# Merge gate logits of layer 2: projected in 128-column blocks inside the stick-breaking heads

## The chip, the cores and the metric

The kernel runs on 1 core of a Trainium2 chip. Its time is the device time of one launch in microseconds. Times quoted as "us from the start" are positions in one profiled execution. Engines are named as the profile names them: PE (TensorE matmuls), DVE (VectorE), ACT (ScalarE), POOL (GpSimd), SP (the queue that issues the DMAs).

## The reference, cut to what matters

Two transformer layers over 1024 tokens of width 1024, in float32. Only layer 2 is touched:

```
h = rms_norm(x)
sb_q, sb_k, sb_v, sb_g, r_q, r_k, r_v, r_g, m_sb, m_ret = split(h @ w_in)   # 10 x 1024 columns
out_a = stick_breaking(norm(sb_q), norm(sb_k), sb_v) * silu(sb_g)           # 8 heads of 128
out_b = norm(chunkwise_retention(rot(r_q), rot(r_k), r_v)) * silu(r_g)      # 4 heads of 256
merged = sigmoid(m_sb + b0) * (out_a @ w_branch_sb) + sigmoid(m_ret + b1) * (out_b @ w_branch_ret)
x = x + merged @ w_out
```

The merge gate logits are `m_sb` and `m_ret` with their biases: 2048 columns of the input projection. They depend on `h` alone and are needed only when the branches are merged.

## The kernel before

Every float32 product is made of three matmul passes over a rounded part and a rest of both operands (`PASSES`), so a block of 128 columns over 512 tokens takes 8 x 3 = 24 matmuls. Weights come in eight tiles of 128 rows (`split_unit`): a DMA into `raw` (three buffers), then POOL makes the rounded part (L70) and the rest (L71) in `wu` (ten buffers). Projection sums land in three PSUM banks named `acc`.

Layer 2 goes in five steps. **Heads:** for each of 8 stick-breaking heads, `dense_tok` projects q, k, v of 8 token tiles (L102, 192 matmuls 384 wide) and `dense_col` the gate (L112, 48 matmuls 512 wide). Then come 12 score blocks of a head (`pz`, L1025), each followed by a long elementwise chain over ACT, DVE and POOL (L1028 to L1048), transposes of the weights (`pt`, `pp`, L1055) and the value products (`po`, L1060). **Logits 0:** `merge_logits(0)` projects the first 512 of the 2048 logit columns, adds the bias on ACT (L956) and stores them in DRAM (`d_sg`). **Retention:** for each of 4 heads a projection (`ret_proj`) and a recurrence over 8 chunks (`ret_chain`, L1132 to L1187), which works on chunk 1 only after chunk 0. **Logits 1 to 3:** the other 1536 columns. **Merge:** `gated` multiplies the heads' outputs with their gates (L1201 to L1215, 16 half tiles through two buffers `ga` and two `oa`), `w_branch_sb` is applied (`acc<-oah,wu`), the same for retention, then `w_out`.

The order in which an engine takes its instructions is fixed when the program is built: a scheduler lists them by priority in the order in which they are written, and where an operand isn't ready in its model it takes later work first. Each engine then runs its own list strictly in order, so a waiting instruction holds up those behind it. A pool's memory is handed to a later pool only when the tiles that lie there are released. `gated` uses pools made after the retention's pool `rt` is closed.

Of the kernel before, what the change touches and what calls it, by code (L numbers as in the profile page):

```python
# [11 lines left out]
F32 = mybir.dt.float32  # L12
F32R = mybir.dt.float32r
AF = mybir.ActivationFunctionType
ALU = mybir.AluOpType
AX = mybir.AxisListType
PSUM = bass.MemoryType.PSUM
DRAM = bass.MemoryType.DRAM

P = 128  # L20
T = 1024
# [6 lines left out]
def f32(ap):  # L28
    return ap.bitcast(F32)
# [7 lines left out]
def tile_kernel(ctx: ExitStack, tc: tile.TileContext, I: dict, out: bass.AP, dbg=None, stop=None):  # L37
    nc = tc.nc
# [20 lines left out]

    # ---------------------------------------------------------------- helpers  # L60
    def split_unit(src, ncol, pool=None, tag="wu", parts=1, fast=False, rpool=None):
# [66 lines left out]
    def dve_transpose(dst, src):  # L128
        """dst[c, x, r, t] = src[t, x, r, c], 128 by 128 for every x and r, in blocks of 32 by 32"""
        for a in range(4):  # L130
            for b in range(4):
                nc.vector.transpose(out=dst[32 * b:32 * b + 32, :, :, 32 * a:32 * a + 32],  # L132
                                    in_=src[32 * a:32 * a + 32, :, :, 32 * b:32 * b + 32])
# [40 lines left out]
    def drain(g):  # L174
        for _ in g:
            pass

    def take(g, n):
        for _ in range(n):
            if next(g, None) is None:  # L180
                return
# [5 lines left out]

    # DRAM scratch
    d_pk = dram.tile([2, NM, P, 4, 4, P], F32, name="d_pk")
# [12 lines left out]

    # ---------------------------------------------------------------- layer 1: norm
    hT = join(new_halves("h1", 0), new_halves("h1", 1))
# [26 lines left out]

    # constants
    conv_w = load_const("conv_w", [P, 12, 5])
# [5 lines left out]
    dnw = load_const("dn_norm_w", [P, P], src=I["dn_norm_w"].partition_broadcast(P))  # L239
    # ---------------------------------------------------------------- layer 1: dz + gates  # L240
    gates = sm.tile([P, NM, 16], F32, name="gates")
# [23 lines left out]

    # gate scalars, [token in chunk, dir*4+head, chunk]
    gt = gates.rearrange("p m (d c h) -> p d c h m", d=2, c=2)
# [30 lines left out]

    # ---------------------------------------------------------------- layer 1: delta heads
    dn_ = tc.tile_pool(name="dn", bufs=1, side="right")  # L300
# [3 lines left out]
    for h in range(4):  # L304
# [5 lines left out]
        for b in range(3):  # L310
# [13 lines left out]
            sT.append(s)  # L324
        # q: raw, with its norm per token
        sq = dc.tile([P, T], F32, tag="cv", name="sq", bufs=2)
# [6 lines left out]
        nc.vector.tensor_scalar_mul(out=rq[:, h, :], in0=rq[:, h, :], scalar1=P ** -0.5)  # L333
        # k: token major, normalized, and back
        ks = dn.tile([P, NM], F32, tag="ks", name="ks", bufs=2)
# [31 lines left out]
        for d in range(2):  # L367
# [12 lines left out]

            # decay [s, c]: with its diagonal for the products with q, strictly above it for the system
            # (the backward system is stored transposed)
            def decay(a, b, sgn, strict, tag):
# [11 lines left out]
            else:  # L395
# [17 lines left out]
                for g in range(2):  # L413
# [5 lines left out]
                    for dd_, E in enumerate((E0, E1)):  # L419
# [3 lines left out]
                        nc.sync.dma_start(out=d_pk[dd_, g * 4:g * 4 + 4, :, 3, h, :].rearrange("n p c -> p n c"), in_=IT)  # L423
        # operands of the scan
        for d in range(2):
# [21 lines left out]

    # ---------------------------------------------------------------- layer 1: inverses of the 64-blocks
    naB = tc.tile_pool(name="naB", bufs=1, side="right")
# [26 lines left out]

    # ---------------------------------------------------------------- layer 1: neighbourhood attention

    def na_proj(p, hold):
# [13 lines left out]
        for m, acc in dense_tok(hT, us, 0, 384):  # L493
            j = m % 4
            sq = na1.tile([P, 256], F32, tag="sq", name="sq", bufs=2)
            nc.scalar.activation(out=sq, in_=acc[:, 0:256], func=AF.Square)
            ss = na1.tile([P, 4], F32, tag="ss", name="ss", bufs=2)
            nc.vector.tensor_reduce(out=ss, in_=sq.rearrange("p (h d) -> p h d", h=4), op=ALU.add, axis=AX.X)
            rsqrt_small(ss, ss, 1.0 / 64, EPS, 4)
            kn = na1.tile([P, P], F32, tag="kn", name="kn", bufs=5)  # L500
            nc.scalar.copy(out=qn[:, m, :], in_=acc[:, 0:128])
            nc.scalar.copy(out=kn, in_=acc[:, 128:256])
            nc.scalar.copy(out=v[:, m, :], in_=acc[:, 256:384])
            for x, t_ in enumerate((qn[:, m, :], kn)):
                t_ = t_.rearrange("p (h d) -> p h d", h=2)
                nc.vector.tensor_tensor(out=t_, in0=t_, in1=ss[:, 2 * x:2 * x + 2].unsqueeze(2).to_broadcast([P, 2, 64]),
                                        op=ALU.mult)
            kns.append(kn)
            if j == 3:
                sl = slice((m - 3) * P, (m + 1) * P)  # L510
                # head 0 keeps its rounded part above the rest, head 1 the other way round
                pt = bank("a")
                for jj, k_ in enumerate(kns):
                    nc.tensor.transpose(pt[:, jj * P:(jj + 1) * P], k_, ident)
                for hh in range(2):
                    a, b = slice(hh * 64, hh * 64 + 64), slice(64 - hh * 64, 128 - hh * 64)
                    nc.scalar.activation(out=kS[hh][a, sl], in_=pt[a, :], func=AF.Copy, scale=gk[a])
                    nc.vector.scalar_tensor_tensor(out=kS[hh][b, sl], in0=pt[a, :], scalar=gk[a],  # L518
                                                   in1=f32(kS[hh][a, sl]), op0=ALU.mult, op1=ALU.subtract)
                kns = []  # L520
            yield 1
# [4 lines left out]
    def na_attn(p, tiles):  # L526
        qn, kS, v, z, TB = tiles[p]

        def scores(t, hh, st):
# [24 lines left out]
            if rl != ru:  # L554
                # the second row's window starts one row later: its last row takes the place of the first
                nc.tensor.matmul(ps[64:128, 0:64], lhsT=q2[:, hh, :], rhs=f32(kS[hh][:, (rl + 8) * 64:(rl + 9) * 64]),
                                 start=True, stop=True)
# [92 lines left out]

    # ---------------------------------------------------------------- layer 1: delta rule scan
    sc_ = tc.tile_pool(name="sc", bufs=1)
# [191 lines left out]

    # ---------------------------------------------------------------- layer 1: output (transposed), layer 2: norm
    # the tokens in two sets: the inner 512, which the scan leaves first, and the outer 512
    def token_set(ap, s):
# [33 lines left out]
    h2T = new_hT(hp2, "h2")  # L881
# [57 lines left out]

    # ---------------------------------------------------------------- layer 2: stick breaking attention  # L940
    NOSYNC = mybir.DependencyInfo(mybir.DependencyClass.NoSync, mybir.DependencyReason.DATA)
# [8 lines left out]

    def merge_logits(q):
        us = load_units(I["w_in_2"], 8192 + 512 * q, 512)
        for b in range(4):
            for half, acc in enumerate(dense_col(h2T, us, b * P)):
                lg = mp.tile([P, 512], F32, tag="lg", name="lg", bufs=2)
                nc.scalar.activation(out=lg, in_=acc, func=AF.Identity, bias=bm[:, 4 * q + b:4 * q + b + 1])  # L956
                nc.sync.dma_start(out=d_sg[4 * q + b, :, half * 512:half * 512 + 512], in_=lg)

# [5 lines left out]
    last_sb = None  # L964
    with tc.tile_pool(name="sb", bufs=1) as sb, tc.tile_pool(name="sr", bufs=1, side="right") as sr:
        gqk = sr.tile([P, 2, P], F32, name="gqk")
# [3 lines left out]
        for h in range(8):  # L970
# [43 lines left out]
            for ib in (0,1):  # L1014
                po = bank("o")
                ini = sb.tile([P, 4], F32, tag="ini", name="ini", bufs=2)
                for diag in ((True, False) if ib else (True,)):
                    c0 = ib * 512 if diag else 0
                    As = []
                    for i4 in range(4):  # L1020
# [27 lines left out]
                        last_sb = nc.scalar.activation(out=A[:, :w], in_=A[:, :w], func=AF.Exp)  # L1048
                        As.append(A)
                    for kb in range(4):  # L1050
                        i0 = kb if diag else 0
# [12 lines left out]
                nc.vector.tensor_copy(out=ov, in_=po)  # L1064
                nc.sync.dma_start(out=d_oa[h, :, ib * 512:ib * 512 + 512], in_=ov)
    if "oa" in dbg:
        nc.sync.dma_start(out=dbg["oa"], in_=d_oa)
    if stop == "E":
        return

    merge_logits(0)

    # ---------------------------------------------------------------- layer 2: retention
    d_ob = dram.tile([8, P, T], F32, name="d_ob")
    d_gb = dram.tile([8, P, T], F32, name="d_gb")
    with tc.tile_pool(name="rt", bufs=1) as rt:
# [45 lines left out]
        def ret_chain(h, tiles):  # L1122
            qTs, kTs, vs = tiles
            state = None
            for g in range(2):
                qT, kT, v = qTs[g], kTs[g], vs[g]
                # scores^T of four chunks
                psc = bank("z")
# [60 lines left out]
        for h in range(4):  # L1189
            ret_chain(h, ret_proj(h))  # L1190
    for q in range(1, 4):
        merge_logits(q)
    if stop == "F":
        return

    # ---------------------------------------------------------------- layer 2: branches and merge
    d_mg = dram.tile([8, P, T], F32, name="d_mg")
# [134 lines left out]
```

## Time and profile before

| | |
|---|---|
| runs | 2332.72 us median of 3 (2330.21 to 2334.63) |
| span of the profiled execution, first to last instruction | 2331.9 us |
| PE busy | 2182.4 us, 94% |
| DVE busy | 1414.8 us, 61% |
| ACT busy | 863.7 us, 37% |
| POOL busy | 1252.0 us, 54% |
| mean granted TensorE clock | 0.981 of full |

Of the profiled execution its span is given; what lies around it is within the spread of the three runs. PE's busy time counts a matmul from its start to its modelled end. Matmuls overlap: one 512 wide is shown as 0.39 us long, but the next starts 0.23 us after it. So PE's true idle time is larger than its share suggests, and it is found by counting matmuls and multiplying with the distance between starts.

### The profile page before, as it was taken

The numbers are of one execution on the slowest core, as the hardware profiler recorded it, in microseconds if no ns is written. First come the engines' busy times: TensorE is split into PE (matmuls) and PEld (weight loads), VectorE is DVE, ScalarE is ACT, GpSimd is POOL, SyncE is SP. The second block draws the span as 40 slices with busy tenths as digits, with TensorE's granted clock in tenths as the row PEclk, the third lists the DMA queues.
The fourth block names the chain that finished last, engine by engine and source line by source line (L and its number), as shares of the span: only waits on it lengthen the run. The fifth ranks groups of instructions, "written<-read, shape, count | busy, mean of one in ns | idle before, by whom it ended". The sixth has DMA issues, their size and how long they took to land.

```text
span 2331.9 us, 33715 instructions
## 1 busy us (share of the span) xinstructions
PE 2182.4 (94%) x12069; PEld 1864.4 (80%) x12069; DVE 1414.8 (61%) x2596; ACT 863.7 (37%) x2126; POOL 1252.0 (54%) x1467
## 2 busy tenths in 40 slices
PE   7998888999999999899889999999999999989999
PEld 7776877787888798787788777788888888767887
DVE  4688789844456568887877784426474744343221
ACT  5344334445554235554555544112222222332210
POOL 6667778851004256565565664536363633666531
PEclk9999999999999999999999999999999999999999
DMA  4266820154475421111011112211111122666433
GB/s 131 80 170 166 203 80 26 37 165 132 154 279 205 153 84 46 50 55 55 10 50 50 55 50 72 72 56 46 64 46 64 46 82 91 226 213 211 140 109 108
DMA packets 236488, 240.86 MB, mean 103 GB/s; under 512 B 39776, under 2 KB 173600, under 8 KB 236064
## 3 DMA queue, kind: packets, MB, share of 16 engines
q1 hardware_dynamic: 236320, 238.71, 32.5%
q8 instruction: 95, 1.56, 0.3%
q14 instruction: 73, 0.60, 0.1%
HBM read 167.31 MB, written 71.34 MB: 102 GB/s over the span
## 4 chain that ended last, share of the span: by engine, by line
PE 33%; DVE 16%; POOL 7%; issue 4%; DMA 4%; ACT 4%; SPq 0%; POOLq 0%; ACTq 0%; DVEq 0%
PE acc L112 21%; PE acc L102 5%; DVE qf L132 4%; PE acc L859 3%; DVE A L1039 3%; POOL A L1044 2%; DMA raw<-in_w_in_dram 1%; POOL wu L71 1%; DVE A L1035 1%; POOL ss L126 1%; DMA oa<-d_oa 1%; DVE ob L132 1%; DVE sq L988 1%; DVE wT L1058 1%; PE pt L1160 1%
## 5 line engine op out<-in xcount | busy, mean ns | idle before, releaser
L112 PE MATMUL acc<-h2h,wu 128*128 128x512 f32 x1504 | 459.1, 396 | 6.7 <-DVE sq L988 2.7
L102 PE MATMUL acc<-wu,h2h 128*128 128x384 f32 (+1 forms) x1536 | 376.2, 327 | 13.4 <-DVE sq L988 4.2
L71 POOL TENSOR_TENSOR wu<-raw,wu 128x512 fp32r<-128x512 f32 (+3 forms) x268 | 363.4, 1365 | 6.3
L70 POOL TENSOR_SCALAR wu<-raw 128x512 fp32r<-128x512 f32 (+3 forms) x268 | 205.9, 772 | 250.7 <-PE acc L112 176.7
L112 PEld LDWEIGHTS acc<-h2h,wu 128*128 128x128 f32 x1504 | 281.5, 188 | 71.9 <-ACT lg L956 3.1
L102 PEld LDWEIGHTS acc<-wu,h2h 128*128 128x128 f32 x1536 | 272.2, 194 | 21.5 <-issue 3.5
L112 PE MATMUL acc<-h2l,wu 128*128 128x512 f32 x752 | 276.1, 396 | 0.0
L102 PE MATMUL acc<-wu,h2l 128*128 128x384 f32 (+1 forms) x768 | 250.1, 327 | 0.0
L102 PE MATMUL acc<-wu,h1hi 128*128 128x384 f32 (+2 forms) x768 | 193.1, 335 | 12.6 <-DVE kS L518 6.7
L112 PE MATMUL acc<-h1hi,wu 128*128 128x512 f32 x512 | 164.3, 409 | 8.0 <-ACT pad L315 4.7
L112 PEld LDWEIGHTS acc<-h2l,wu 128*128 128x128 f32 x752 | 141.4, 188 | 31.0
L102 PEld LDWEIGHTS acc<-wu,h1hi 128*128 128x128 f32 x768 | 138.5, 196 | 17.0 <-issue 8.0
L1044 POOL TENSOR_TENSOR A<-Z,A 128x128 f32<-128x128 f32 (+2 forms) x96 | 112.4, 1176 | 70.5 <-DVE A L1039 43.6
L102 PEld LDWEIGHTS acc<-wu,h2l 128*128 128x128 f32 x768 | 148.4, 193 | 1.0
L102 PE MATMUL acc<-wu,h1lo 128*128 128x384 f32 (+2 forms) x384 | 127.8, 335 | 0.0
L112 PEld LDWEIGHTS acc<-h1hi,wu 128*128 128x128 f32 x512 | 98.1, 193 | 33.0 <-ACT pad L315 6.2
L126 POOL TENSOR_TENSOR ss<-ss,mhalf 128x2 f32<-128x2 f32 (+2 forms) x136 | 115.6, 851 | 7.2
L132 DVE STREAM_TRANSPOSE qf<-sq 32x256 f32<-32x256 f32 x256 | 111.6, 436 | 4.0
L125 POOL TENSOR_SCALAR ss<-ss 128x2 f32<-128x2 f32 (+2 forms) x136 | 42.5, 312 | 117.7 <-ACT sq L982 47.0
L1060 PE MATMUL po<-wT,v 128*128 128x512 f32 (+3 forms) x288 | 76.1, 365 | 22.2 <-DVE wT L1058 12.2
L112 PE MATMUL acc<-h1lo,wu 128*128 128x512 f32 x256 | 96.4, 405 | 0.0
L112 PE MATMUL acc<-oah,wu 128*128 128x512 f32 x256 | 81.3, 413 | 10.0 <-DVE sg L1232 6.1
(547 smaller groups left out, 4770.5 us busy)
## 6 DMA issues: line engine op xcount, KB each, us to landing
raw<-in_w_in_dram SPq DMA_DIRECT2D x192, 256.0 KB, 2.8
d_pk<-sct SPq DMA_DIRECT2D x24, 512.0 KB, 4.3
raw<-in_w_out_dram SPq DMA_DIRECT2D x40, 256.0 KB, 2.8
wsa<-d_pk SPq DMA_DIRECT2D x16, 512.0 KB, 6.0
wsb<-d_pk SPq DMA_DIRECT2D x16, 512.0 KB, 7.1
d_sg<-lg SPq DMA_DIRECT2D x32, 256.0 KB, 2.6
sg<-d_sg SPq DMA_DIRECT2D x32, 256.0 KB, 4.3
raw<-in_w_in_dram SPq DMA_DIRECT2D x32, 192.0 KB, 2.7
```

Source lines behind the costliest of these rows:

```text
L70: nc.gpsimd.tensor_scalar(out=u[:, 0, :], in0=raw, scalar1=1.0, scalar2=0.0, op0=ALU.mult, op1=ALU.add)
L71: nc.gpsimd.tensor_tensor(out=u[:, 1, :], in0=raw, in1=f32(u[:, 0, :]), op=ALU.subtract)
L102: nc.tensor.matmul(acc[:, :n], lhsT=hT[a][:, k, m * P:(m + 1) * P], rhs=us[k][:, b, c0:c0 + n], start=(k == 0 and i == 0), stop=(k == NK - ...
L112: nc.tensor.matmul(accs[half], lhsT=us[k][:, b, c0:c0 + P], rhs=hT[a][:, k, half * 512:(half + 1) * 512], start=(k == 0 and i == 0), stop= ...
L125: nc.gpsimd.tensor_scalar(out=dst, in0=src, scalar1=mul, scalar2=eps, op0=ALU.mult, op1=ALU.add)
L126: nc.gpsimd.tensor_tensor(out=dst, in0=dst, in1=mhalf[:, :eshape], op=ALU.pow)
L132: nc.vector.transpose(out=dst[32 * b:32 * b + 32, :, :, 32 * a:32 * a + 32], in_=src[32 * a:32 * a + 32, :, :, 32 * b:32 * b + 32])
L859: nc.tensor.matmul(acc, lhsT=us[k][:, y, (b % 4) * P:(b % 4 + 1) * P], rhs=token_set(mT[x][:, k, 0:T], s), start=(k == 0 and i == 0), stop ...
L988: nc.vector.scalar_tensor_tensor(out=sq[:, a * P:(a + 1) * P], in0=acc[:, a * P:(a + 1) * P], scalar=ss[:, a:a + 1], in1=gqk[:, a, :], op0 ...
L1039: nc.vector.tensor_tensor_scan(out=A[:, :w][:, ::-1], data0=A[:, :w][:, ::-1], data1=A[:, :w][:, ::-1], initial=0.0 if diag else ini[:, i4 ...
L1044: nc.gpsimd.tensor_tensor(out=A[:, :w], in0=Z[:, :w], in1=A[:, :w], op=ALU.subtract)
L1060: nc.tensor.matmul(po[:, i0 * P:512], lhsT=v[a][:, c0 // P + kb, :], rhs=wT[b][:, :n], start=(diag and kb == 0 and x == 0), stop=(diag == ...
```

## The change

`merge_logits` becomes a generator over 16 blocks of 128 columns. A block loads its weights in two DMAs of 4 row tiles (`fraw`, two buffers), splits them on POOL (`fu`, three buffers, L960 and L961 of the new file) and yields after each half of 512 tokens. Every head asks for one half after the scores of each of its three groups of four blocks, 24 halves in all; the other 8 follow after the last head. Both former calls are gone. The same edit sets the size of a scratch reserve (`dynamic_dma_scratch_size`) to 1024. The count of matmuls is the same.

```diff
-    def merge_logits(q):
-        us = load_units(I["w_in_2"], 8192 + 512 * q, 512)
-        for b in range(4):
-            for half, acc in enumerate(dense_col(h2T, us, b * P)):
+    def merge_logits():
+
+        for b in range(16):
+            cols = slice(8192 + b * P, 8192 + (b + 1) * P)
+            us = []
+            for g in range(2):
+                raw = fp.tile([P, 4, P], F32, tag="fraw", name="fraw", bufs=2)
+                nc.sync.dma_start(out=raw, in_=I["w_in_2"][g * 512:(g + 1) * 512, cols].rearrange("(k p) c -> p k c", p=P))
+                u = fp.tile([P, 2, 4, P], F32R, tag="fu", name="fu", bufs=3)
+                nc.gpsimd.tensor_scalar(out=u[:, 0], in0=raw, scalar1=1.0, scalar2=0.0, op0=ALU.mult, op1=ALU.add)
+                nc.gpsimd.tensor_tensor(out=u[:, 1], in0=raw, in1=f32(u[:, 0]), op=ALU.subtract)
+                us += [u[:, :, k, :] for k in range(4)]
+            for half in range(2):
+                acc = dense_half(h2T, us, 0, half)
                 lg = mp.tile([P, 512], F32, tag="lg", name="lg", bufs=2)
-                nc.scalar.activation(out=lg, in_=acc, func=AF.Identity, bias=bm[:, 4 * q + b:4 * q + b + 1])
-                nc.sync.dma_start(out=d_sg[4 * q + b, :, half * 512:half * 512 + 512], in_=lg)
+                nc.scalar.activation(out=lg, in_=acc, func=AF.Identity, bias=bm[:, b:b + 1])
+                nc.sync.dma_start(out=d_sg[b, :, half * 512:half * 512 + 512], in_=lg)
+                yield 1
...
+        fill = merge_logits()
...
                         last_sb = nc.scalar.activation(out=A[:, :w], in_=A[:, :w], func=AF.Exp)
                         As.append(A)
+                    take(fill, 1)
...
+        drain(fill)
...
-    merge_logits(0)
...
-    for q in range(1, 4):
-        merge_logits(q)
...
-    nc = _bacc.Bacc("TRN2", target_bir_lowering=False, num_devices=1)
+    nc = _bacc.Bacc("TRN2", target_bir_lowering=False, num_devices=1, dynamic_dma_scratch_size=1024)
```

How it stands on PE in the scores of a middle head, before: between the score blocks `pz` lie projections of the next head (`acc<-wu`, 384 wide).

```order
L1025 MATMUL pz<-qkt 128x256 x3
L1025 MATMUL pz<-qkt 128x384 x3
L102 MATMUL acc<-wu,h2h 128x384
L102 MATMUL acc<-wu,h2l 128x384
L102 MATMUL acc<-wu,h2h 128x384 x2
L102 MATMUL acc<-wu,h2l 128x384
L1055 MATMUL pt<-ident,A 128x128
L1055 MATMUL pp<-ident,A 128x128
L102 MATMUL acc<-wu,h2h 128x384
```

The same place after the change: between the score blocks lie the logit matmuls (`acc<-h2h,fu`).

```order
L1038 MATMUL pz<-qkt 128x384 x3
L120 MATMUL acc<-h2h,fu 128x512
L120 MATMUL acc<-h2l,fu 128x512
L120 MATMUL acc<-h2h,fu 128x512 x2
L120 MATMUL acc<-h2l,fu 128x512
L120 MATMUL acc<-h2h,fu 128x512 x2
L1038 MATMUL pz<-qkt 128x512 x3
L120 MATMUL acc<-h2l,fu 128x512
L120 MATMUL acc<-h2h,fu 128x512 x2
L120 MATMUL acc<-h2l,fu 128x512
L120 MATMUL acc<-h2h,fu 128x512
L1069 MATMUL pt<-ident,A 128x128
```

The logits stand among the scores, and most of the next head's projection now stands behind them, among the value products.

On PE at the end of the last retention head, before: logits (`acc<-h2h,wu`) lie between the state products (`po<-v,kd`) and the outputs of a chunk (`pt<-v,wT` and `pt<-ss,qs`).

```order
L1171 MATMUL po<-v,kd 128x256 x6
L112 MATMUL acc<-h2l,wu 128x512
L112 MATMUL acc<-h2h,wu 128x512 x2
L112 MATMUL acc<-h2l,wu 128x512
L112 MATMUL acc<-h2h,wu 128x512 x2
L112 MATMUL acc<-h2l,wu 128x512
L112 MATMUL acc<-h2h,wu 128x512
L1152 MATMUL pt<-v,wT 128x256 x3
L1160 MATMUL pt<-ss__18692,qs 128x256
```

The same after the change, up to the first matmul on the gated output `oah`.

```order
L1173 MATMUL pt<-ss__19488,qs 128x256
L1173 MATMUL pt<-ss__19489,qs 128x256
L1173 MATMUL pt<-ss__19488,qs 128x256 x2
L1173 MATMUL pt<-ss__19489,qs 128x256
L1173 MATMUL pt<-ss__19488,qs 128x256
L1165 MATMUL pt<-v,wT 128x256 x3
L1173 MATMUL pt<-ss__19519,qs 128x256
L1173 MATMUL pt<-ss__19520,qs 128x256
L1173 MATMUL pt<-ss__19519,qs 128x256 x2
L1173 MATMUL pt<-ss__19520,qs 128x256
L1173 MATMUL pt<-ss__19519,qs 128x256
L112 MATMUL acc<-oah,wu 128x512
```

The logits between the chunks of the last retention head, and between it and the first branch matmul, are gone.

On SP after the change, where the loads of the first gated half tiles (`ga`, `oa`) stand: behind the last stores of the retention's outputs (`d_ob`), as before the change, but now with the branch weights already loaded ahead of them.

```order
L64 DMA raw<-in_w_branch_sb_dram 128x512 x5
L1200 DMA d_ob<-ob 128x512 x4
L1218 DMA ga<-d_ga 128x512
L1219 DMA oa<-d_oa 128x512
L1218 DMA ga<-d_ga 128x512
L1219 DMA oa<-d_oa 128x512
```

The gating still starts only when the last retention head has ended.

## Rows read from the trace of the kernel before

**Rows 1.** Windows by step: span, busy (and count) by engine, clock, DMA share, GB/s

```profile
886.50:1451.10 564.60, 513.62 (x2679) 450.22 (x2678) 441.74 (x847) 288.55 (x832) 336.30 (x439) 0.98 0.15 45
...
1890.00:1981.50 91.50, 91.50 (x446) 76.20 (x446) 40.14 (x73) 22.49 (x48) 37.22 (x47) 1.00 0.27 91
1981.50:2063.00 81.50, 73.23 (x306) 56.34 (x304) 32.82 (x33) 29.38 (x48) 56.04 (x47) 1.00 0.64 213
2063.00:2149.50 86.50, 79.76 (x318) 62.33 (x319) 38.38 (x47) 27.78 (x45) 48.61 (x40) 0.94 0.65 216
2149.50:2331.90 182.40, 178.69 (x768) 143.70 (x766) 36.57 (x50) 19.08 (x31) 72.75 (x71) 1.00 0.36 124
```

**Rows 2.** PE's groups from 886.5 to 1451.1 us: count, busy, mean ns, idle before

```profile
L102 PE MATMUL acc<-wu,h2h 128*128 128x384 f32 x860 | 234.1, 346 | 9.3 <-DVE sq L988 3.6 <-DVE wu L68 2.5 <-ACT gv L1012 2.3
...
L112 PE MATMUL acc<-h2h,wu 128*128 128x512 f32 x350 | 109.9, 397 | 2.7 <-DVE sq L988 2.7
L1060 PE MATMUL po<-wT,v 128*128 128x512 f32 (+3 forms) x288 | 76.1, 365 | 22.2 <-DVE wT L1058 12.2 <-ACT wT L1057 4.5 <-DVE ov L1064 1.7
L1025 PE MATMUL pz<-qkt 128*128 128x512 f32 (+3 forms) x288 | 71.3, 358 | 10.0 <-ACT Z L1028 7.8 <-ACT qkt L999 2.1
...
L1055 PE MATMUL pt<-ident,A 128*128 128x128 f32 x160 | 33.8, 282 | 6.8 <-ACT A L1048 6.7
```

**Rows 3.** PE's timeline at three places: start, length of the run, its count

```profile
1166.09 0.69 PE L102 MATMUL acc<-wu,h2h 128*128 128x384 f32 x3
...
1888.37 1.95 PE L1132 MATMUL pz<-ro 128*128 128x128 f32 x16
...
2077.24 1.10 PE L112 MATMUL acc<-oah,wu 128*128 128x512 f32 x4
```

**Rows 4.** PE's timeline in the last retention head, two chunks

```profile
1909.52 0.51 PE L1152 MATMUL pt<-v,wT 128*128 128x256 f32 x3
...
1917.80 0.52 PE L1152 MATMUL pt<-v,wT 128*128 128x256 f32 x3
```

**Rows 5.** DVE's and POOL's timeline in the same head

```profile
1913.28 0.55 DVE L1165 TENSOR_SCALAR ot<-pt,rdv,ss 128x256 f32<-128x256 f32 x1 [0.45 <-POOL ss L126]
...
1922.13 7.18 DVE L132 STREAM_TRANSPOSE ob<-ot 32x256 f32<-32x256 f32 x16
...
1932.87 7.18 DVE L132 STREAM_TRANSPOSE kf<-ro 32x256 f32<-32x256 f32 x16 [0.24 <-DMA d_ob<-ob]
...
1970.45 7.19 DVE L132 STREAM_TRANSPOSE ob<-ot 32x256 f32<-32x256 f32 x16
...
1912.30 0.94 POOL L126 TENSOR_TENSOR ss<-ss,mhalf 128x1 f32<-128x1 f32 x1
```

**Rows 6.** Instructions on tile oa: ns min/median/max, first and last start

```profile
L1209 POOL TENSOR_TENSOR oa<-oa,ga x32: 1271/1297/1793, 1985.9 to 2137.0; 128x512 f32<-128x512 f32 x32
L1213 DVE TENSOR_TENSOR oa<-oa,ga x32: 691/781/1699, 1987.9 to 2139.0; 128x512 f32<-128x512 f32 x32
...
L1214 ACT CAST oah<-oa x16: 612/620/623, 1988.6 to 2060.7; 128x512 fp32r<-128x512 f32 x16
```

**Rows 7.** DMA issues from 1980 to 2070 us: median us to landing

```profile
oa<-d_oa SPq DMA_DIRECT2D x16, 256.0 KB, 3.4
```

**Rows 8.** A window at the start of the retention, columns as in rows 1

```profile
1510.00:1520.70 10.70, 8.35 (x40) 7.95 (x40) 8.74 (x18) 1.66 (x2) 3.83 (x4) 0.53 0.17 51
```

**Rows 9.** PE's timeline in that window, at half clock

```profile
1516.41 0.41 PE L102 MATMUL acc<-wu,h2l 128*128 128x256 f32 x1
1516.62 0.63 PE L102 MATMUL acc<-wu,h2h 128*128 128x256 f32 x2
```

**Rows 10.** POOL's weight splits on the page: mean ns, idle before

```profile
L71 POOL TENSOR_TENSOR wu<-raw,wu 128x512 fp32r<-128x512 f32 (+3 forms) x268 | 363.4, 1365 | 6.3
L70 POOL TENSOR_SCALAR wu<-raw 128x512 fp32r<-128x512 f32 (+3 forms) x268 | 205.9, 772 | 250.7 <-PE acc L112 176.7
```

More of the change, by code (lines that the diff above doesn't have):

```diff
@@ L964, in tile_kernel @@
     last_sb = None
-    with tc.tile_pool(name="sb", bufs=1) as sb, tc.tile_pool(name="sr", bufs=1, side="right") as sr:
+    with tc.tile_pool(name="fp", bufs=1) as fp, tc.tile_pool(name="sb", bufs=1) as sb, \
+            tc.tile_pool(name="sr", bufs=1, side="right") as sr:
+        fill = merge_logits()
         gqk = sr.tile([P, 2, P], F32, name="gqk")
```

## Prediction

> **What bounds the kernel now.** I read the page first: PE is the busiest engine, DVE second, and the end of the chain of waits is mostly PE. Then the windows by step, because the change moves work from two steps into a third. The reader is to see in them that the steps have different limits [rows 1]: in the heads (886.5 to 1451.1 us) PE is shown busy for 513.62 of 564.60 us while DVE works 441.74, or 78%; in the last retention head (1890.0 to 1981.5) PE is busy all the time and DVE 44%; in the gating (1981.5 to 2063.0) PE still has 73.23 of 81.50 us. The PE work of those last two windows is for the most part logits 1 to 3.
>
> Then the groups of PE in the heads, to count the matmuls [rows 2]: 860 on `h2h` 384 wide, with half as many on `h2l` (two passes of three read `h2h`), so 1290; 350 and half as many 512 wide, some 524; 288 each of `po`, `pz` and transposes. Their distance comes from runs in the timeline [rows 3]: four 512 wide take 1.10 us, one alone 0.40, so 0.233 each; three 384 wide 0.69 against 0.34, so 0.175; sixteen 128 wide 1.95, so 0.11. Of `po` and `pz` half are 512 wide and a sixth each 384, 256 and 128 (256 wide: 0.117, from three in 0.51 us against 0.28 for one [rows 4]). The sum is 1290 x 0.175 = 226, 524 x 0.233 = 122, 2 x (144 x 0.233 + 48 x (0.175 + 0.117 + 0.11)) = 106 and 288 x 0.11 = 32, together 486 us. So PE waits 564.6 - 486 = 79 us in this step. That is what the change can win there.
>
> The groups also tell where PE waits [rows 2]. Of 51 us shown idle, 22.2 stand ahead of `po` (for the weights `wT` of DVE and ACT), 10.0 ahead of `pz`, 6.8 ahead of `pt`, 12.0 ahead of projections.
>
> **The change part by part.** *What moves.* 32 halves of 24 matmuls, 768, at 0.233: 179 us of PE. 192 of them (logits 0, 45 us) already lie in the window of the heads and still do, as the eight halves drained at the end. The other 576, or 134 us, come from beside the last retention head and the gating into the heads. No matmul is added or dropped.
>
> *The heads get longer.* They grow by 134 us less what falls into the 79 us of waiting. The bounds are 134 - 79 = 55 (every wait filled) and 134 (none). In the new order the logits lie between the score blocks, and the projections behind them among the value products. So the waits ahead of `pz` and `pt` get cover; those ahead of `po` lie among the same neighbours as before. I let the share of `po` stay: 79 x 22.2 / 51 = 34 us. The projection waits go, since most stood behind DVE, whose 442 us would then lie in some 654 (67%). The heads grow by 134 - 79 + 34 = 89 us.
>
> *The last retention head loses its cover.* What is left is the recurrence itself, and it gets faster, because PE no longer runs logits between its links. A chunk took 8.28 us from one `pt` to the next [rows 4]. Its links are the nine matmuls from 1909.52, ACT's square, POOL's root until 1913.24 and DVE's `ot` until 1913.83 [rows 5], when the bank is free again: 4.4 us. The transposes of DVE between the two halves of the sequence and at the end (7.18 us three times [rows 5]) stay as they are. In the first half three steps save 3.9 us each, so its last `ot` would end at 1910 and not at 1922, where the transposes follow it. From there to the first state of the second half I keep the 25 us of before (two rows of transposes, the store between them, the split of `kd`). The last three chunks save 10: two steps, and some 2 us in which the first of them stood behind logits. So 91.5 us become 70 at full clock.
>
> The clock speaks against it. In a window with PE waiting and a granted clock of 0.53 [rows 8], two matmuls 256 wide take 0.63 us against 0.41 for one, a distance of 0.21 to 0.22 [rows 9], and not 0.117. Nine matmuls of a chunk then cost 0.9 us more, eight chunks 7 us. With some hundred short matmuls in 70 us I expect the lower level (1.2 GHz): 77 us, 14.5 less than before. Bounds: 70 and, if the links are no faster, 91.5. The Trainium skill says the same of the cause, in TensorE: Matmul & The Clock Gate (Part 1: The HAM clock gate): the reduced clock is the default and sustained activity releases it. No row shows this recurrence bare; by the rule its matmuls run at half rate, 77 us; with the clock held up it would be 70.
>
> *The gating loses its cover too.* It takes 81.5 us [rows 1]; its last cast starts at 2060.7 and its first at 1988.6 [rows 6], 4.8 us per half tile. Two buffers let two halves share one round: 3.4 us to landing [rows 7], POOL 1.30, DVE twice 0.69 or more, ACT's cast 0.62 and its sigmoid, of the same shape, as much [rows 6]; together 7.3, or 3.65 per half. That gives 58 us as the lower bound; the upper one is 81.5. Logit stores and weight loads no longer stand on the same queues. I take 65, nearer to the lower: 16.5 less.
>
> *The first branch product.* Its 384 matmuls need 89 us. Before, 86.5 us passed after the gating [rows 1]. Bare, the first 48 follow the gating tile by tile and end with it, which leaves 336 x 0.233 = 78, plus some 5 for a start at half clock and the odd wait: 85, or 1.5 less. What follows (182.4 us) is as before.
>
> *At no cost.* The eight logits' ACT and store instructions per block stay and lie on engines with room (ACT 51% in the heads). The weight splits on POOL stay in number. 24 tiles' worth move into the heads at 0.77 + 1.37 us [rows 10], 51 us on top of 336; POOL is then 59% busy there. If that cover goes, PE waits for a `fu` tile, and behind a split that waits stand POOL's subtraction and selects of the score chain; this is priced in a rival.
>
> Two-input DVE instructions of one shape take from 0.69 to 1.70 us [rows 6]. The Trainium skill, SBUF — State Buffer (SBUF: two separate sides), gives a cause: GpSimd and such a VectorE instruction share a port pair, and whoever holds it blocks the other for the whole instruction. By that rule at most the moved 51 us are added to DVE's 442, or 493 of some 654 us: 75%, no more than its 78% now. The trace agrees with the spread; the sum stays, and the rule only lends weight to the rival below in which the waits stay.
>
> *The sum:* 2331.9 + 89 - 14.5 - 16.5 - 1.5 = 2388 us. The span of the profiled execution lies 0.8 us below the median of the runs, so nothing is added for it: 2389.
>
> **The rivals.**
> *All waits are filled* (25%). For it: where matmuls stand without a chain between them PE hardly waits, 3.7 us in the last 182 [rows 1], and PE would be the most loaded engine in the heads, 620 of 640 us. Against it: `po` waits for weights made two instructions earlier, whatever lies in other places. The heads grow by 60, the tail gives back 32: 2360.
> *The waits stay or new ones come* (17%). For it: `fu` has three buffers and a block needs two, so the second half of a block's weights is split only when the block before is nearly done, on a POOL that also carries the score chain. Against it: DVE and POOL have more time per head than before. The heads grow by 134, the tail gives back 32: 2434.
> *Faster* (6%): the bare tail is far cheaper than priced. The mechanism is the gating at the pace of its busy engines and not of its round: if landing is hidden, a half tile costs DVE, ACT and POOL some 3 us, 16 of them 48; with the recurrence at 65 and all waits filled, 55 - 26 - 33 - 3 gives 2325. It decides when recurrence and gating together fall under 115 us, where I have 142 and before had 173. Against it: the landing of 3.4 us is inside a round of two buffers, and no row has the round shorter.
> The rest of the chance (my own case) is 52%.
>
> **How the numbers follow.** A measurement of this kernel tells some 0.2%, or 5 us, from no change. My own case covers 2365 to 2415; the range reaches to the rival with all waits filled and to most of the one where they stay: 2348 to 2432, leaving out some 9% on either side. Faster holds 6%; no change 4%, from the edge between the filled rival and the faster one; slower the rest, 90%.
>
> **What would show it.** In the changed profile: some 650 us from the first score of head 0 to the last value product, with the idle time ahead of `pz` and `pt` mostly gone and that ahead of `po` left; a bare last recurrence of 70 to 80 us with a clock near 0.5, in steps of 4.4 to 5.3 us; after it a gating of 60 to 70 us with PE nearly idle; from there an end as before. I am wrong if the gating starts before the last store of the retention, if the recurrence keeps its 8.3 us steps, if the heads end within 20 us of where they did, or if PE waits for `fu`.

## The result and the profile after

The changed kernel takes 2389.76 us (median of 4 runs, 2384.19 to 2397.69) against 2333.68 of the kernel before: ratio 1.0233, interval 1.0206 to 1.026. 2389 was predicted. The span of the profiled execution is 2390.0 us.

The page shows in its row of 40 slices where the time went. A slice of the changed kernel is 59.75 us, a digit the busy share in tenths, for PEclk the granted clock. First the row of the kernel before, then the two of the changed one:

```profile
PE   7998888999999999899889999999999999989999
...
PE   7998888999999999999999999999999994478999
PEclk9999999999999999999999999999999996579999
```

In the changed kernel PE reads 9 from the eighth slice to the 33rd. Then come two slices with 4 and one with 7, at a lower clock. Before, the same places read 9, 9 and 8, since logits lay there. The windows by step (columns as in [rows 1]; first the heads, then the stretch up to the bare recurrence, the recurrence, the gating, the first branch product, the rest):

```profile
889.80:1543.10 653.30, 631.04 (x3252) 551.11 (x3251) 474.36 (x847) 304.22 (x856) 401.02 (x490) 1.00 0.19 59
1543.10:1984.70 441.60, 428.12 (x2395) 373.11 (x2394) 233.61 (x393) 89.19 (x199) 214.45 (x222) 0.98 0.17 55
1984.70:2057.10 72.40, 23.34 (x105) 20.11 (x103) 38.10 (x73) 13.91 (x34) 20.49 (x31) 0.59 0.11 41
2057.10:2121.70 64.60, 34.69 (x71) 20.10 (x72) 25.09 (x34) 22.49 (x36) 21.53 (x16) 0.55 0.50 165
2121.70:2207.10 85.40, 77.00 (x315) 60.10 (x314) 35.22 (x46) 28.41 (x46) 45.26 (x38) 0.97 0.63 211
2207.10:2390.00 182.90, 178.92 (x769) 144.29 (x767) 36.82 (x50) 19.20 (x31) 72.97 (x71) 1.00 0.36 124
```

Against [rows 1] the heads grew by 88.7 us (564.6 to 653.3), the recurrence lost 19.1 (91.5 to 72.4), the gating 16.9 (81.5 to 64.6), the branch product 1.1, and the rest gained 0.5. The first score starts 3.3 us later (889.8 against 886.5) and the stretch between heads and recurrence is 2.7 longer (441.6 against 438.9). Together that is +58.1, the difference of the two spans. So 134 us of PE work left the two tail steps, and these gave back 36: they were held up by chains that the logits had merely filled.

PE's groups in the heads, as in [rows 2] (count, busy, mean ns, idle before and its releasers):

```profile
L102 PE MATMUL acc<-wu,h2h 128*128 128x384 f32 x896 | 241.9, 343 | 4.1 <-DVE sq L1001 4.1
L120 PE MATMUL acc<-h2h,fu 128*128 128x512 f32 x472 | 156.0, 400 | 0.3 <-POOL fu L961 0.3
...
L1074 PE MATMUL po<-wT,v 128*128 128x512 f32 (+3 forms) x288 | 71.8, 351 | 10.5 <-DVE wT L1072 7.9 <-ACT wT L1071 1.6 <-DVE ov L1078 0.9
L1038 PE MATMUL pz<-qkt 128*128 128x512 f32 (+3 forms) x288 | 69.7, 354 | 2.0 <-ACT Z L1041 1.8
...
L1069 PE MATMUL pt<-ident,A 128*128 128x128 f32 x160 | 32.8, 282 | 5.4 <-ACT A L1061 5.4
```

The idle time ahead of `pz` fell from 10.0 to 2.0 us and that ahead of the projections from 12.0 to 4.4; that ahead of `po` halved (22.2 to 10.5), and that ahead of `pt` hardly moved (6.8 to 5.4). PE waits 0.3 us for `fu`.

### The profile page after: what moved, and what is told of

The parts are those of the page before. It is cut to its first block, busy times and chain, and to the rows that moved or that the text cites. A ratio compares the mean times of both kernels' runs of the same rounds, so it can differ in the third digit from the quotient of the medians.

```text
span 2390.0 us, 33754 instructions
## 1 busy us (share of the span) xinstructions
PE 2196.3 (92%) x12069; PEld 1874.5 (78%) x12069; DVE 1432.2 (60%) x2596; ACT 864.8 (36%) x2126; POOL 1257.1 (53%) x1467
## 4 chain that ended last, share of the span: by engine, by line
PE 37%; DVE 12%; POOL 9%; issue 4%; DMA 3%; ACT 3%; SPq 0%; POOLq 0%; ACTq 0%; DVEq 0%
PE acc L112 17%; PE acc L102 8%; PE acc L120 4%; PE acc L859 3%; DVE qf L132 3%; POOL A L1057 2%; DVE A L1052 2%; POOL wu L71 1%; PE po L1074 1%; DVE ob L132 1%; POOL ss L126 1%; DMA oa<-d_oa 1%; DVE kf L132 1%; PE pt L1173 1%; POOL wu L70 1%
## 5 line engine op out<-in xcount | busy, mean ns | idle before, releaser
L71 POOL TENSOR_TENSOR wu<-raw,wu 128x512 fp32r<-128x512 f32 (+3 forms) x236 | 319.5, 1362 | 4.7
L70 POOL TENSOR_SCALAR wu<-raw 128x512 fp32r<-128x512 f32 (+3 forms) x236 | 179.5, 764 | 247.2 <-PE acc L112 178.1
L112 PE MATMUL acc<-h2h,wu 128*128 128x512 f32 x992 | 302.8, 395 | 0.0
L112 PEld LDWEIGHTS acc<-h2h,wu 128*128 128x128 f32 x992 | 185.9, 188 | 41.8
L112 PE MATMUL acc<-h2l,wu 128*128 128x512 f32 x496 | 183.0, 395 | 0.0
L120 PE MATMUL acc<-h2h,fu 128*128 128x512 f32 x512 | 168.7, 399 | 0.3 <-POOL fu L961 0.3
L112 PE MATMUL acc<-oah,wu 128*128 128x512 f32 x256 | 93.3, 453 | 51.2 <-DMA xi<-d_x 21.6
L125 POOL TENSOR_SCALAR ss<-ss 128x2 f32<-128x2 f32 (+2 forms) x136 | 36.7, 270 | 157.2 <-ACT sq L995 83.9
L120 PEld LDWEIGHTS acc<-h2h,fu 128*128 128x128 f32 x512 | 95.5, 188 | 22.1 <-POOL fu L961 1.6
L112 PEld LDWEIGHTS acc<-oah,wu 128*128 128x128 f32 x256 | 54.2, 216 | 71.1 <-ACT oah L1225 26.7
```

Of the source, the lines that this page charges most:

```text
L70: nc.gpsimd.tensor_scalar(out=u[:, 0, :], in0=raw, scalar1=1.0, scalar2=0.0, op0=ALU.mult, op1=ALU.add)
L71: nc.gpsimd.tensor_tensor(out=u[:, 1, :], in0=raw, in1=f32(u[:, 0, :]), op=ALU.subtract)
L112: nc.tensor.matmul(accs[half], lhsT=us[k][:, b, c0:c0 + P], rhs=hT[a][:, k, half * 512:(half + 1) * 512], start=(k == 0 and i == 0), stop= ...
L120: nc.tensor.matmul(acc, lhsT=us[k][:, b, c0:c0 + P], rhs=hT[a][:, k, half * 512:(half + 1) * 512], start=(k == 0 and i == 0), stop=(k == N ...
L125: nc.gpsimd.tensor_scalar(out=dst, in0=src, scalar1=mul, scalar2=eps, op0=ALU.mult, op1=ALU.add)
```

## The experiments

Ten kernels were run, each against the kernel before. The first four tell where the 134 us are worth what; the next four ask why; the last two try the clock and a version that is faster than both.

**The tail without its logits.** The kernel before, with the matmuls of logits 1 to 3 left out, and with them the loads and splits of their weights:

```diff
-        us = load_units(I["w_in_2"], 8192 + 512 * q, 512)
+        us = load_units(I["w_in_2"], 8192 + 512 * q, 512) if q == 0 else None
...
-            for half, acc in enumerate(dense_col(h2T, us, b * P)):
+            for half, acc in enumerate(dense_col(h2T, us, b * P) if q == 0 else (h2T[0][:, 0, 0:512], h2T[0][:, 1, 0:512])):
```

> The kernel before with logits 1 to 3 not projected; their stores are kept, from other data. My theory: the last retention head and the gating take some 72 and 65 us when nothing lies beside them, so of the 134 us of PE work that goes only some 37 come back: 2296 us. Rival (the tail is bound by PE, and the loss of the change lies in the heads alone): all 134 us come back, 2200 us.

Measured: 2301.59 us, ratio 0.9858 (0.9839 to 0.9877). Its windows of recurrence and gating:

```profile
1896.00:1968.60 72.60, 21.74 (x93) 18.77 (x92) 34.85 (x69) 28.98 (x57) 18.09 (x28) 0.57 0.32 116
1968.60:2030.00 61.40, 31.23 (x67) 17.46 (x68) 23.25 (x31) 21.98 (x35) 21.50 (x16) 0.64 0.53 167
```

134 us of PE work taken out of the program altogether win 33 us. The two bare steps take 134 us, nearly as in the changed kernel (137). So what the tail gives back doesn't depend on the heads.

**Both.** The changed kernel, with logits 1 to 3 projected a second time behind the retention, where they stood before:

```diff
+    for q in range(1, 4):
+        old_logits(q)
```

> The changed kernel in which logits 1 to 3 are projected a second time where they stood before (576 matmuls twice). My theory: the heads grow as in the changed kernel, by 95 us, and the tail is that of the kernel before, so 2333 + 95 = 2428 us, 38 above the changed kernel. Rival (the heads take the logits nearly for nothing and the loss is the bare tail): 2340 to 2350 us.

Measured: 2430.92 us, ratio 1.041 (1.0393 to 1.0427). Recurrence and gating are back at 89.7 and 83.3 us in its windows, and the heads keep their 653 (heads, recurrence, gating):

```profile
887.90:1541.00 653.10, 629.66 (x3252) 549.77 (x3251) 473.63 (x847) 304.39 (x856) 400.90 (x490) 1.00 0.19 60
1985.00:2074.70 89.70, 89.70 (x437) 74.70 (x436) 37.88 (x72) 22.23 (x48) 35.62 (x45) 1.00 0.27 87
2074.70:2158.00 83.30, 75.04 (x306) 57.60 (x304) 33.92 (x32) 29.64 (x48) 54.27 (x46) 0.98 0.64 207
```

So what the heads lose and what the tail gives back are independent sums.

**Eight and twelve of the sixteen blocks moved.** With eight, a head takes one half and eight halves are drained; with twelve, it takes two:

```diff
-        for b in range(16):
+        for b in range(8):
...
-                    take(fill, 1)
+                    if diag and not ib:
+                        take(fill, 1)
...
+    for q in range(2, 4):
+        old_logits(q)
```

> Half of the blocks moved: one half block per head and eight after the heads; logits 2 and 3 stay behind the retention. My theory, by interpolation: the heads grow by 20 to 31 us, the last retention head stays covered, the gating loses 16: 2337 to 2348 us. Rival (the first logits in the heads fall into waits and cost nothing): the heads grow by under 8, 2325 us, faster than both.

> Three quarters moved: two half blocks per head and eight after the heads; logits 3 stay behind the retention. My theory: the heads grow by 51 to 62 us, the tail gives back some 26: 2358 to 2369 us. Rival (each block moved costs the same less the waits that are still there): above 2369 us, or, if the waits go first, under 2350 us.

Measured: 2343.7 us (ratio 1.0039, 1.0024 to 1.0054) and 2372.02 us (1.016, 1.0145 to 1.0175). The first is what was expected; the second lies above its range, with its rival. The windows of the heads, first eight, then twelve blocks:

```profile
887.80:1476.10 588.30, 554.32 (x2878) 487.15 (x2877) 443.95 (x847) 293.46 (x840) 360.90 (x458) 0.99 0.16 52
```

```profile
892.10:1517.30 625.20, 594.46 (x3070) 519.71 (x3069) 460.81 (x847) 301.77 (x848) 376.06 (x474) 0.99 0.18 55
```

With 0, 8, 16 and 24 halves moved, the matmuls counted in the windows of the heads are 486, 530.6, 574 and 616.5 us of PE work at the prediction's distances. (In the changed kernel these are 1344 matmuls 384 wide and 1044 512 wide beside those of the scores, transposes and values; 60 of the 768 logit matmuls lie outside of the window.) So PE waits 79, 58, 51 and 37 us: each step of eight halves, 43 to 45 us, fills 21, 7 and 14 us of waiting. From the end of the heads to the end of the kernel it takes 880.8, 866.8, 855.9 and 846.9 us: each 45 us taken from the tail give back 14, 11 and 9. No step pays here, the first loses least.

**Four buffers for the gating.** The gating's pace was said to be the round of two buffers. One size is changed, in the changed kernel and in the one before (there with the scratch reserve set to 1024, as in the change):

```diff
-                ga = mg.tile([P, 512], F32, tag="ga", name="ga", bufs=2)
-                oa = mg.tile([P, 512], F32, tag="oa", name="oa", bufs=2)
+                ga = mg.tile([P, 512], F32, tag="ga", name="ga", bufs=4)
+                oa = mg.tile([P, 512], F32, tag="oa", name="oa", bufs=4)
```

> The changed kernel with four buffers instead of two for the loaded tiles ga and oa of the gating. My theory: the bare gating goes at the pace of the round of a buffer (landing of oa, POOL, DVE, ACT: 3.65 us per half tile), and with four buffers at the pace of its busiest engine, some 2 us of DVE per half: the gating falls from 64.6 to about 40 us and the time to some 2365 us (2358 to 2374). Rival: the round is not what binds; POOL's products or the order of the queues do, and the gating stays within 5 us of 65, the time at 2385 to 2393.

> The kernel before with four buffers for ga and oa (and 1 KB of the room for dynamic DMA given up, to make place). My theory: before the change PE's logits fill the gating (73 of 81.5 us busy), so the round of the buffers is hidden behind them for the most part: at most the 8 us in which PE waits come back, 2324 to 2334 us. Rival: the gating was bound by its buffers there too, and the time falls by as much as in the changed kernel, some 25 us, to 2308.

Measured: 2371.26 us (ratio 1.0151, 1.0133 to 1.0168) in the changed kernel, 2336.0 us (0.9991, 0.9981 to 1.0001) in the one before. The windows of the gating in the changed kernel with four buffers, and then of gating and branch product in the kernel before with four:

```profile
2059.80:2102.00 42.20, 24.78 (x57) 16.22 (x58) 27.30 (x28) 19.80 (x33) 21.33 (x15) 0.62 0.72 242
```

```profile
1989.40:2052.00 62.60, 54.99 (x220) 43.03 (x219) 38.93 (x34) 28.33 (x47) 48.36 (x35) 0.95 0.80 262
2052.00:2155.30 103.30, 96.17 (x404) 76.21 (x403) 42.83 (x45) 27.53 (x46) 58.81 (x52) 0.97 0.56 190
```

The bare gating falls by 22 us and the kernel by 18. The kernel before stays where it was, above the 2324 to 2334 expected; so the scratch reserve of 1024, which it has here, costs nothing that shows. Its gating falls too, from 81.5 to 62.6, and the branch product grows from 86.5 to 103.3: PE's logits are only done later. The same edit is worth 0.8% on one side of the change and nothing that can be told on the other. The round of two buffers can be read from ACT's timeline in the changed kernel, the casts of four half tiles:

```profile
2079.84 0.62 ACT L1225 CAST oah<-oa 128x512 fp32r<-128x512 f32 x1 [0.76 <-DVE oa L1224]
2082.35 0.62 ACT L1225 CAST oah<-oa 128x512 fp32r<-128x512 f32 x1 [0.76 <-DVE oa L1224]
2086.97 0.62 ACT L1225 CAST oah<-oa 128x512 fp32r<-128x512 f32 x1 [0.76 <-DVE oa L1224]
2089.58 0.62 ACT L1225 CAST oah<-oa 128x512 fp32r<-128x512 f32 x1 [0.76 <-DVE oa L1224]
```

They come in pairs, these 7.1 to 7.2 us apart; 7.3 was worked out. From the first of the 16 casts (2065.1) to the last (2119.8) it is 3.65 us per half, as in the prediction. The landing in that round was 2.8 us where 3.4 went into the sum, so some 0.6 us of it lie elsewhere than the sum had them.

**The weight splits beside DVE.** In the heads DVE is busy 474.36 us after the change and 441.74 before [rows 1], with the same 847 instructions. This kernel loads and splits the weights of one block only and uses them for all 16:

```diff
-            us = []
-            for g in range(2):
+            if b == 0:
+                us = []
+            for g in range(2 if b == 0 else 0):
```

> The changed kernel, but the weights of all 16 blocks of logits are those of block 0, loaded and split once: 30 of the 32 weight tiles' loads and POOL splits are left out (the logits 1 to 15 of the output are not the reference's). DVE was busy 474 us in the heads after the change and 442 before, with the same 847 instructions. My theory: VectorE is held up by the splits on POOL beside it; without them its busy time in the heads falls back to 440 to 450 us, and the waits of PE there by 5 to 15 us: 2374 to 2385 us. Rival: the splits hold up nobody, DVE is busy longer only because the heads are longer; its time stays at 465 to 480 us and the kernel at 2387 to 2393. Second rival: POOL's queue is what PE waits for in the heads; they fall by 25 us or more, below 2365.

Measured: 2382.52 us, ratio 1.0197 (1.0172 to 1.0223); the interval overlaps that of the changed kernel, so the time alone doesn't tell it from the rival. Its window of the heads does, in part:

```profile
890.40:1533.50 643.10, 621.74 (x3228) 546.59 (x3227) 453.22 (x847) 303.81 (x855) 325.82 (x431) 1.00 0.15 49
```

DVE is busy 21 us less than in the changed kernel, not 24 to 34 as expected, and the heads are 10 us shorter. The scheduler also listed PE's instructions in another order in this kernel. Its logit matmuls in that window are 684 (456 and 228), not 708 (472 and 236), that is one half of 24 less:

```profile
L120 PE MATMUL acc<-h2h,fu 128*128 128x512 f32 x456 | 150.4, 398 | 0.0
L120 PE MATMUL acc<-h2l,fu 128*128 128x512 f32 x228 | 91.0, 399 | 0.0
```

So 5.6 of the 10 us only moved behind the window. By counted matmuls PE waits 32 us in these heads and 37 in the changed kernel's: some 5 us are left, and the other order may have a part in them. The direct evidence is in two timelines of the changed kernel, DVE's and POOL's:

```profile
1131.03 0.23 DVE L1043 TENSOR_SCALAR A<-Z 128x128 f32<-128x128 f32 x1
...
1145.62 1.31 DVE L1043 TENSOR_SCALAR A<-Z 128x128 f32<-128x128 f32 x1
```

```profile
1143.67 1.48 POOL L961 TENSOR_TENSOR fu<-fraw,fu 128x512 fp32r<-128x512 f32 x1
1145.11 1.74 POOL L71 TENSOR_TENSOR wu<-raw,wu 128x512 fp32r<-128x512 f32 x1
```

The same form of DVE instruction takes 0.23 us while POOL is idle (between 1130.2 and 1131.7) and 1.31 us when it starts inside a split: it ends at 1146.93, the split at 1146.85. The Trainium skill, SBUF — State Buffer (SBUF: two separate sides), has a rule for this: GpSimd and a VectorE instruction in a mode with two ports, or with two inputs in SBUF, share a port pair, and the one that comes second waits for the other's whole instruction. The ends in the trace agree with it; in which mode this one-input instruction ran, the trace doesn't tell.

**The logits in finer pieces.** In the changed kernel a half of 24 matmuls was issued in four pieces of six, the later ones among the value products:

```diff
-                    take(fill, 1)
                     for si, A in enumerate(As):
...
+                        take(fill, 1)
```

> The changed kernel with the same logits in pieces: each half of 24 matmuls is issued in four pieces of six, the first part ahead of the value products and the others between them, ahead of the transposes that make the next weights wT. My theory: what is left of PE's waits in the heads (some 39 us, the most of it ahead of po and pt) stands inside the value part, where a piece of 1.4 us put in the right place covers it: the heads fall by 10 to 20 us, 2370 to 2380 us. Rival: the chain score, cumulated sums, weights of DVE and ACT sets the pace there and pieces only delay its next link: no gain, 2387 to 2400 us.

Measured: 2394.08 us, ratio 1.0243 (1.0227 to 1.026). The number agrees with the rival, but the experiment says nothing on it: PE's matmuls in the heads stand in the same order as in the changed kernel, and the window is as long (653.1 us). The scheduler, which lists by readiness, came to the same list from both texts. Whether the waits left ahead of `po` and `pt` could be filled stays open.

**The clock of the bare recurrence.** Six matmuls 512 wide, whose result nobody reads, in seven chunks of the last retention head:

```diff
+                    if h == 3 and n > 0:
+                        warm = bank("a")
+                        for x in range(6):
+                            nc.tensor.matmul(warm, lhsT=qs[0][:, 0, :], rhs=h2T[0][:, 1, 0:512], start=(x == 0), stop=(x == 5))
```

> The changed kernel with six more matmuls 512 wide, whose results nobody reads, behind those of po in the seven later chunks of the last retention head, to keep TensorE at the full clock there. My theory: the bare recurrence runs at a granted clock near 0.5 because PE waits most of the time; if the six (1.4 us at full clock) raise it, a step falls from 5.1 towards 4.4 us and the recurrence by 3 to 7 us: 2382 to 2388 us. Rival: six are too few, the clock stays at 0.5 and they take 2.5 us each time on the path to the next state: the steps grow to 6 us or more and the time to 2395 or more. Second rival: the clock decides nothing there, since the links are those of ACT, POOL and DVE: the same time within 3 us, with a raised clock.

Measured: 2385.2 us, ratio 1.0222 (1.0203 to 1.0241), not to be told from the changed kernel's 1.0233. The trace tells what the time can't. The chunks' first matmuls in the changed kernel (PE's timeline; in brackets the idle time before):

```profile
1985.51 0.52 PE L1165 MATMUL pt<-v,wT 128*128 128x256 f32 x3
1991.92 1.01 PE L1165 MATMUL pt<-v,wT 128*128 128x256 f32 x3 [3.31 <-DVE ot L1178]
1998.53 0.84 PE L1165 MATMUL pt<-v,wT 128*128 128x256 f32 x3
2003.68 0.80 PE L1165 MATMUL pt<-v,wT 128*128 128x256 f32 x3 [3.02 <-DVE ot L1178]
2008.77 1.01 PE L1165 MATMUL pt<-v,wT 128*128 128x256 f32 x3 [3.02 <-DVE ot L1178]
```

and with the six:

```profile
1993.21 0.63 PE L1165 MATMUL pt<-v,wT 128*128 128x256 f32 x3 [0.54 <-DVE ot L1182]
1997.68 0.62 PE L1165 MATMUL pt<-v,wT 128*128 128x256 f32 x3 [1.02 <-DVE ot L1182]
2002.12 0.62 PE L1165 MATMUL pt<-v,wT 128*128 128x256 f32 x3 [1.03 <-DVE ot L1182]
```

A step falls from 5.09 to 4.44 us, and the windows of the two stretches, first the changed kernel's, show granted clocks of 0.55 and 1.00, the two levels (1.2 and 2.4 GHz) nearly pure:

```profile
2003.00:2013.00 10.00, 4.37 (x18) 3.78 (x18) 6.55 (x14) 1.78 (x5) 2.62 (x5) 0.55 0.00 0
1993.20:2007.00 13.80, 9.41 (x51) 7.16 (x51) 8.50 (x17) 3.17 (x9) 4.47 (x7) 1.00 0.00 0
```

But few steps are of this kind. From the first chunk to the last it takes 56.4 us in the one and 54.8 in the other: the two intervals with transposes (10.5 and 18.0 us) are as long in both, and the first step is 1.2 us longer with the six. So the recurrence gains 1.7 us, not the 3 to 7 expected; that is nearer to the second rival.

**A version that is faster than both.** Eight blocks moved, and four buffers (the same for `oa`):

```diff
-                ga = mg.tile([P, 512], F32, tag="ga", name="ga", bufs=2)
+                ga = mg.tile([P, 512], F32, tag="ga", name="ga", bufs=4)
```

> Eight of the blocks of logits moved (one half per head between the score blocks, the others at the end of the heads), logits 2 and 3 behind the retention as before, and four buffers for ga and oa. My theory: with eight blocks moved the gating is bare for the most part (62 us between 2017 and 2079 in the trace of that kernel with two buffers), so the buffers that brought nothing to the kernel before bring some 20 us here: 2316 to 2328 us, less than the kernel before. Rival: the gain of the four buffers needs a gating that is wholly bare; with logits left in its first 10 us it is under 8 us, and the time stays at 2334 or more.

Measured: 2329.89 us (8 runs, 2326.16 to 2332.09) against 2336.3, ratio 0.9969 (0.9957 to 0.9982). It is 0.3% under the kernel before, just above the range expected (2316 to 2328), and 0.7% under its like with two buffers (ratio 1.0039), some 16 us where 16 to 28 were expected. The groups of PE on the first tiles `oah`, from the pages with two and then with four buffers:

```profile
L112 PE MATMUL acc<-oah,wu 128*128 128x512 f32 x256 | 92.2, 445 | 32.4 <-ACT oah L1236 25.7
```

```profile
L112 PE MATMUL acc<-oah,wu 128*128 128x512 f32 x256 | 88.2, 435 | 17.0 <-ACT oah L1236 9.5
```

The idle time ahead of them falls by 15 us. Why the other 17 stay was not looked into.

## Why the prediction was right, and where it was not

*The balance, by its steps.* Heads +89 predicted, +88.7 measured. Gating 65 and 64.6, branch product 85 and 85.4, the rest unchanged but for 0.5. The recurrence was put at 77 and took 72.4. Against these 4.6 us too many stand 3.3 us by which the first score came later and 2.7 between heads and recurrence, neither of them in the sum. The 3.3 are within the spread of executions: the changed kernel, its version with four buffers and that of the clock have the same code up to there, and their traces have the first score at 889.8, 893.0 and 887.2 us. So the steps are right, but that the total is right to a microsecond is luck. (The prediction says that nothing is added to its sum of 2388 for the 0.8 us between span and runs, and yet gives 2389.)

*The waits in the heads: near in size, wrong in place.* The prediction let the waits ahead of `po` stay and had those ahead of `pz`, `pt` and the projections go; that came to 34 us, and 37 are left by the same distances. But the `po` share halved, and the `pt` share and a third of the projections' stayed. The step "those ahead of `po` lie among the same neighbours as before" failed; the prediction's own sentence before it has the projections among the value products. That the parts cancel to 37 is luck, and so is part of the +88.7: 130.5 us of PE work came into the window and not 134, and 42 us of waiting went and not 45. What covered the waits ahead of `po` isn't shown: between transposes and the next value product stand some 810 matmuls of projections where there were some 690, but fewer of gates and logits. The runs with eight and twelve blocks show the same: 21, 7 and 14 us filled by equal pieces is no rule of a fixed share.

*DVE's time was taken as fixed.* "442 us would then lie in some 654" became 474. The bound given, 51 us on top, held. What these 33 us cost in waits is not settled: the kernel without the splits gives some 5, in another order of PE's matmuls.

*The bare recurrence.* The later steps go as worked out, 5.1 us where 5.3 was the estimate, and at the lower level of the clock (0.55). The term that was too large is the half clock: 7 us were charged for eight chunks, and the run with the full clock in the steps gained 1.7. On the other side the first two steps took 6.4 and 6.6 us, for reasons that the prediction didn't name. In the first it is POOL. ACT's square is done at 1986.7, but the first link of the chunk's root (`ss`, L125) stands behind splits of the branch weights until 1989.88, and one more split lies between it and the second link:

```profile
1986.85 2.94 POOL L71 TENSOR_TENSOR wu<-raw,wu 128x512 fp32r<-128x512 f32 x2
1989.88 0.19 POOL L125 TENSOR_SCALAR ss<-ss 128x1 f32<-128x1 f32 x1
1990.15 0.62 POOL L70 TENSOR_SCALAR wu<-raw 128x512 fp32r<-128x512 f32 x1
1990.73 0.55 POOL L126 TENSOR_TENSOR ss<-ss,mhalf 128x1 f32<-128x1 f32 x1
```

In the later chunks the two links follow each other at once (0.19 and 0.95 us), and in the second step they do so too. There it is PE: `ot` is done at 1997.4, but six state products, which waited for DVE's `st`, stand ahead of the next outputs:

```profile
1997.12 1.62 PE L1184 MATMUL po<-v,kd 128*128 128x256 f32 x6 [2.91 <-DVE st L1190]
1998.53 0.84 PE L1165 MATMUL pt<-v,wT 128*128 128x256 f32 x3
```

*The gating.* The lower bound of 58 us, 3.65 per half, is the pace that the casts keep; the first cast comes 8 us after the start. That the round of two buffers is the mechanism is shown: four buffers take 22 us off. The run also shows what the rival "faster" needed: gating and recurrence together took 137 us, and even with four buffers 114 (71.8 and 42.2), just under the 115 from which that rival was to decide. But its other condition, all waits in the heads filled, never came.

*The rivals.* All waits filled: no, 37 us are left. The waits stay: no, 42 of 79 went. That PE would wait for `fu`: 0.3 us.

## What to carry to other kernels

Work that runs beside a chain of dependent steps is worth only what the step takes without it: before moving it away, price the bare step link by link, since a busy engine at 100% may be filling time that something else sets. Work moved into a full stretch costs its whole length less the waits that it covers there, and equal pieces cover unequal waits. Once a step is bare, look for the size that sets its pace: a buffer count that was worth nothing under cover was worth a third of the 56 us that the whole move had lost, and more than the 9 us that half of it had lost.

## What the hardware showed

A one-input DVE instruction (TENSOR_SCALAR on 128x128) took 1.31 us and ended with the split on POOL inside which it had started; with POOL idle it took 0.23 us; the rows of before had shown a spread only for two-input ones [rows 6]. With four buffers in the bare gating the loads of `oa` land later, in the median in 5.0 us where it was 2.8, while the window moves 242 GB/s where it was 165: the round of a buffer gets longer as more of them are under way, and the gating still falls by a third. DMA issues of the changed kernel in the gating, and of the one with four buffers:

```profile
oa<-d_oa SPq DMA_DIRECT2D x16, 256.0 KB, 2.8
```

```profile
oa<-d_oa SPq DMA_DIRECT2D x16, 256.0 KB, 5.0
```
